# A hybrid diffusion trunk in one launch: the residual added by accumulating transfers, bare first sums, and the last stores and weight rows placed behind the operands

## The chip, the core and the metric

The kernel runs on one core of a Trainium2 chip. The metric is the device time of one execution in microseconds; times are given as the median of several runs with the lowest and the highest. A profile is one further execution, taken by the hardware profiler, with its own time.

The engines go by the names of the profile. PE is the matrix engine and PEld its weight load. DVE and ACT are the vector and the scalar engine. POOL and SP here only issue transfers. Each engine, and each queue of transfers, works through its own instructions in order.

## The reference, cut to what matters

One layer works on 640 tokens (512 latent, 128 context) of width 1024: a gated feed-forward half step, a token mixer, and a second half step.

```python
def swiglu(h, w1, w3, w2):
    return (jax.nn.silu(h @ w1) * (h @ w3)) @ w2
...
    x = x + 0.5 * m[2] * swiglu(hh, p['ffn1_w1'][l], p['ffn1_w3'][l], p['ffn1_w2'][l])
    hh = rmsnorm(x, g[1]) * (1 + m[4]) + m[3]
    y, ctx_out = token_mixer(hh, p, l, ctx)
    x = x + m[5] * y
    hh = rmsnorm(x, g[2]) * (1 + m[7]) + m[6]
    x = x + 0.5 * m[8] * swiglu(hh, p['ffn2_w1'][l], p['ffn2_w3'][l], p['ffn2_w2'][l])
```

The nine vectors `m` come from a conditioning vector times a 1024 by 9216 matrix. The inner width of the half steps is 2816. At its end the mixer adds two gated products, `sigmoid(gm) * (hm @ w_br_m) + sigmoid(gd) * (att @ w_br_d)`, and multiplies the sum by `w_out`.

## The kernel before, in words

Everything lies with features on the partitions, and the 640 tokens are two halves of 320 columns. Every product is done in three matmuls: weight and operand are split into a rounded high part and the remainder, and high by high, high by low and low by high are summed in PSUM (`mm3`, L159). ACT makes the high part (tile `ww`, `wB`, `wC` or `wH`), DVE the remainder.

**Half step.** The inner width is 11 blocks of 256. The two up products of a block are one weight granule each. From block 1 on each granule is done in seven products (Winograd's form of Strassen's algorithm, `products`, L375): the two halves of the tokens and of the inner dimension are added and subtracted beforehand, and so are the four quadrants of the weight. `parts` (L259) makes from the raw weight rows the tiles `wB` and `wC`, then the sums in place; `sums` (L277) makes `ww` of them. A product is 12 matmuls where a granule holds four row blocks. ACT copies running sums out of PSUM (`u`, `ps_f<-ps_f`) between the products, and the next product into that bank waits for the copy. The gated result of each block is stored to `g_dram` (`store_g`, L492).

**Down products.** The 11 blocks are summed in three groups, each for four output granules `j` of 256 features. In the first half step (`run_first`, L551) group 0 is blocks 0 to 3, done plainly (per `j` four units of 24 matmuls), group 1 is blocks 4 to 7 in seven products, group 2 the last three, plainly. In the second (`run`, L638) group 0 is blocks 0 to 2, plainly (units of 18 matmuls), and groups 1 and 2 are four blocks each in seven products. The operands of a group are fetched back from `g_dram` by `fetch` into tiles that the up products used (`S`, `hm`) or that lie free (`gA`, `SO`). An operand's fetch therefore waits until PE has used what lay there. Weight rows go to a ring of two `raw` buffers. Each unit's sum is scaled by the gate and added into the residual `x` by DVE (`add_residual`, L225). `x` had been read back to the core as four pairs of 640 KB (L1062 and L2305) while group 0 ran.

**Columns.** The conditioning matrix's columns are done on DVE, in 56 tiles (`Columns`, L730; `tile`, L747): each is a load of 512 KB on POOL's queue into `raw_a` or `ada` and two reductions, which DVE does wherever the program places the tile. At the mixer's end the tiles stand between the 16 units of `w_brd` (24 matmuls each) and the 16 of `w_brm`, with one buffer, so that a load can begin only when the tile before is done. `d_evac` (L2138) empties each `w_brd` unit's bank into `y`.

**What sets the order.** A planner with its own cost model lays down each engine's order; `issue_after` gives it an instruction to stay behind. On the chip each queue is in order and waits by semaphores. SP issues most transfers. POOL issues the column loads and some of the operand fetches, ACT one small load at the start.

## Time and profile before

| | us |
|---|---|
| median of 3 runs (lowest to highest) | 1839.37 (1837.65 to 1842.87) |
| the profiled execution | 1839.15 |
| its span, first to last instruction | 1837.4 |
| PE busy | 1800.9 (98%) |
| DVE busy | 1340.3 (73%) |
| ACT busy | 876.8 (48%) |
| POOL busy | 37.3 (2%) |
| bytes over the span | 166 GB/s, with HBM read 238.14 MB and written 67.56 MB |

A row of the waits says which engine waited for which, how long in total, how often, and the longest. A row of the timeline has the start, the length, engine, line, instruction and count; in brackets stands the idle time before it and what ended it. A row of stretches has its bounds, its length, then the busy time of PE, PEld, DVE, ACT and POOL with counts, the granted clock of PE (1.00 is full), the busy share of the transfer engines, and GB/s.

### The profile page before, as it was taken

To read this page: it belongs to the slowest core of one execution; us is meant where nothing else is said; L and a number is where in the kernel's file an instruction comes from. 1 tells how busy PE (TensorE), PEld (TensorE's weight loads), DVE (VectorE), ACT (ScalarE), POOL (GpSimd) and SP (SyncE) were. 2 spreads that over 40 slices of the span, in tenths; PEclk is the share of its full clock that TensorE was granted. 3 is DMA by queue.
4 is the path that set the end of the run, shared out by engine and by line. 5 is a ranking of instruction groups with operands and counts; after the bars stand their busy time and mean duration, and the time that the engine had idled before them with its cause. 6 is when DMAs were issued, how large, how long until landed. Compare 5 with 4: busy or idle time off the path is not lost. (4 is left out here: it accounts for less than half of the span.)

```text
span 1837.4 us, 30799 instructions
## 1 busy us (share of the span) xinstructions
PE 1800.9 (98%) x12622; PEld 1762.6 (96%) x12622; DVE 1340.3 (73%) x2188; ACT 876.8 (48%) x1510; POOL 37.3 (2%) x67
## 2 busy tenths in 40 slices
PE   8999999989999999999999999999899999999999
PEld 7999999989999999999999989999899999999999
DVE  6888996776986766475485558866767888896575
ACT  5655454123655454455555455672236545543232
POOL 0000000100000000000000000000000000000000
PEclk9999999989999999999999999999999999999999
DMA  8255567955234322112221155665552355658872
GB/s 332 100 197 190 182 218 275 358 212 198 82 137 140 122 67 86 62 62 94 73 91 68 42 165 179 238 213 191 201 173 79 132 173 191 204 187 297 312 292 81
DMA packets 130368, 307.71 MB, mean 167 GB/s; under 512 B 9841, under 2 KB 92017, under 8 KB 117297
## 3 DMA queue, kind: packets, MB, share of 16 engines
q1 hardware_dynamic: 119090, 259.06, 40.7%
q0 software_dynamic: 10992, 46.67, 6.8%
q8 instruction: 99, 1.62, 0.4%
q14 instruction: 43, 0.35, 0.1%
q10 hardware_dynamic: 144, 0.01, 0.0%
HBM read 238.14 MB, written 67.56 MB: 166 GB/s over the span
## 5 line engine op out<-in xcount | busy, mean ns | idle before, releaser
L75 PE MATMUL ps_f<-S,ww 128*128 128x320 f32 x2124 | 341.9, 310 | 2.5 <-DMA S<-g_dram 1.2
L75 PEld LDWEIGHTS ps_f<-S,ww 128*128 128x128 f32 x2124 | 319.1, 188 | 6.0 <-DVE ww L54 4.2
L75 PE MATMUL ps_p<-hH,wH 128*128 128x320 f32 x672 | 213.8, 318 | 6.8 <-DVE y L54 5.9
L75 PE MATMUL ps_f<-hm,ww 128*128 128x320 f32 x1272 | 203.5, 314 | 10.6 <-ACT u L51 6.4
L75 PE MATMUL ps_p<-hL,wH 128*128 128x320 f32 x672 | 208.8, 311 | 0.0
L75 PE MATMUL ps_p<-hH,wL 128*128 128x320 f32 x672 | 208.7, 311 | 0.0
L75 PEld LDWEIGHTS ps_f<-hm,ww 128*128 128x128 f32 x1272 | 193.8, 192 | 11.6 <-ACT u L51 6.6
L75 PE MATMUL ps_t<-wH,hH 128*128 128x256 f32 x640 | 185.2, 289 | 0.9 <-DVE x L57 0.9
L75 PE MATMUL ps_t<-wH,hL 128*128 128x256 f32 x640 | 181.0, 283 | 0.9 <-DVE hL L54 0.9
L75 PE MATMUL ps_t<-wL,hH 128*128 128x256 f32 x640 | 180.8, 283 | 0.0
L54 DVE TENSOR_TENSOR ww<-raw,ww 128x2048 fp32r<-128x2048 f32 (+1 forms) x67 | 150.2, 2241 | 32.9 <-ACT ww L51 32.7
L51 ACT ACTIVATE ww<-raw 128x2048 fp32r<-128x2048 f32 (+1 forms) x67 | 125.3, 1870 | 96.2 <-PE ps_f L75 57.2
L75 PE MATMUL ps_f<-hm,wB 128*128 128x320 f32 x960 | 153.8, 309 | 0.0
L54 DVE TENSOR_TENSOR raw<-raw 128x1024 f32<-128x1024 f32 x168 | 145.2, 864 | 1.8
L75 PEld LDWEIGHTS ps_f<-hm,wB 128*128 128x128 f32 x960 | 144.1, 188 | 0.0
L75 PEld LDWEIGHTS ps_p<-hH,wH 128*128 128x128 f32 x672 | 127.4, 190 | 7.8 <-DVE y L54 6.2
L75 PEld LDWEIGHTS ps_p<-hL,wH 128*128 128x128 f32 x672 | 127.3, 189 | 0.3
L51 ACT ACTIVATE u<-ps_f 128x320 f32<-128x320 f32 x117 | 50.7, 434 | 160.4 <-PE ps_f L75 160.2
L75 PEld LDWEIGHTS ps_p<-hH,wL 128*128 128x128 f32 x672 | 127.2, 189 | 0.0
L75 PEld LDWEIGHTS ps_t<-wH,hH 128*128 128x128 f32 x640 | 122.3, 191 | 1.5 <-ACT nsq L51 1.1
L75 PEld LDWEIGHTS ps_t<-wH,hL 128*128 128x128 f32 x640 | 122.3, 191 | 1.1 <-DVE hL L54 1.1
L75 PEld LDWEIGHTS ps_t<-wL,hH 128*128 128x128 f32 x640 | 122.5, 191 | 0.4
(306 smaller groups left out, 3445.8 us busy)
## 6 DMA issues: line engine op xcount, KB each, us to landing
g_dram<-g SPq DMA_DIRECT2D x44, 640.0 KB, 7.4
raw_a<-in_w_ada_c POOLq DMA_DIRECT2D x30, 512.0 KB, 4.3
g_dram<-g SPq DMA_DIRECT2D x24, 480.0 KB, 8.2
raw<-in_w1b SPq DMA_DIRECT2D x11, 1024.0 KB, 4.8
raw<-in_w3b SPq DMA_DIRECT2D x11, 1024.0 KB, 6.3
raw<-in_w1a SPq DMA_DIRECT2D x10, 1024.0 KB, 4.9
raw<-in_w3a SPq DMA_DIRECT2D x10, 1024.0 KB, 6.2
hm<-g_dram POOLq DMA_DIRECT2D x7, 1280.0 KB, 8.9
```

Source lines behind the costliest of these rows:

```text
L51: return placed(nc.scalar.activation(*args, **kw))
L54: return placed(eng.tensor_tensor(out=out, in0=in0, in1=in1, op=op))
L75: tc.keep_in_program_order(nc.tensor.matmul(*args, **kw))
```

## The change

Five things are altered.

1. `begin_sum` is new. In group 0 of both half steps ACT writes the scaled sum to `x` (a copy with the gate as scale), where DVE added it to a residual that had been read in. The four reads of `x` are gone. In group 1, POOL issues four accumulating transfers (`add_pair`), which add the residual's pairs 2, 3, 0 and 1 into `x`.
2. The stores of the last block, and the weight rows of the second output granule, are issued behind the fetches of group 0's operands. In the first half step these fetches go from POOL's queue to SP's and take another order of tiles.
3. In the first half step, group 1's operands A12 and S3 go from POOL's queue to SP's, A22 and S4 to ACT's queue, behind a copy of the first seven products. Group 2's get both `gA` and `SO`, from SP.
4. The columns are placed differently: 11 tiles in the first up products (10 before), then 9 during group 0 and 4 during group 2 (14 before, some of them during group 1). At the mixer's end 5 and 7 tiles take the place of 6 and 6, with two buffers each, every second unit, and each behind an emptied bank.
5. The weight parts of the next granules are kept behind the last `begin_sum`.

The diff, cut:

```diff
+    def begin_sum(x, ps, d, hf, gate):
+        c0 = hf * HALF
+        for s0, s1, j in SEGS[hf]:
+            ins = act(x[d][:, s0:s1], ps[:, s0 - c0 : s1 - c0], AF.Copy, scale=gate[:, d, j : j + 1])
+        return ins
...
+                    with ExitStack() as st:
+                        st.enter_context(tc.issue_after(gr.split_at))
+                        if i == 0 and self.begun is not None:
+                            st.enter_context(tc.issue_after(self.begun.ins))
                         work[i + 1][0].parts(self.fp)
...
-                    for i in range(2):
-                        nc.sync.dma_start(out=self.g_dram[c0:c1, :, i, b, :].rearrange("s p n -> p s n"), in_=g[:, i].bitcast(F32))
+                    def store(g=g, c0=c0, c1=c1):
+                        for i in range(2):
+                            nc.sync.dma_start(out=self.g_dram[c0:c1, :, i, b, :].rearrange("s p n -> p s n"), in_=g[:, i].bitcast(F32))
+
+                    if b == FB - 1:
+                        self.stores.append(store)
+                    else:
+                        store()
...
-                [up[i] for i in (S1, S2, A11, A12)],
-                [up[i] for i in (S3, S4, A22, S1, S2, A11, A12)],
-                [up[S3], None, up[S1], up[S2]],
+                [up[i] for i in (A11, S1, S2, A12)],
+                [up[i] for i in (S3, S4, A22, A11, S1, S2, A12)],
+                [up[S3], None, None, up[S1]],
...
+            second = down[0][1].load
+            down[0][1].load = lambda: None
+
+            def used_last(i):
+                if i in (A11, S1, S2, A12):
+                    ins = fetch(0, (A11, S1, S2, A12).index(i), nc.sync)
+                    if i == A12:
+                        with tc.issue_after(ins.ins):
+                            second()
+
+            work[-1][3] = used_last
...
+                if q == 0:
+                    self.begun = begin_sum(x, p, 2 * j + f, hf, gate)
+                else:
+                    self.at_vec = add_residual(x, p, 2 * j + f, hf, gate)
...
+                def used(i):
+                    if j == 3 and i in (A11, S3):
+                        fetch(2, {A11: 0, S3: 3}[i])
+                    elif (j, i) == (3, S2):
+                        freed()
...
-                loaded = self.loaded = (down[0][j + 2] if j < 2 else mid[j - 2][0]).load()
-                if 0 < j:
-                    with tc.issue_after(loaded):
-                        fetch(1, (A11, S1, S2)[j - 1], nc.sync)
+                loaded = (down[0][j + 2] if j < 2 else mid[j - 2]).load()
+                with tc.issue_after(loaded):
+                    if j == 0:
+                        for f in self.stores:
+                            f()
+                    for i in ((), (), (A11, S1), (S2,))[j]:
+                        fetch(1, i, nc.sync)
...
-                    mid[0][0].parts(self.fp)
-                    mid[0][0].sums()
+                    with tc.issue_after(self.begun.ins):
+                        mid[0].parts(self.fp)
+                        mid[0].sums()
...
                     if (j, hf) == (3, 0):
-                        fetch(1, A12)
-                        fetch(1, S3)
-            fetch(1, A22)
-            fetch(1, S4)
-
+                        fetch(1, A12, nc.sync)
+                        fetch(1, S3, nc.sync)
...
+                if (i, hf) == (0, 1):
+                    with tc.issue_after(self.copied.ins):
+                        fetch(1, A22, nc.scalar)
+                        fetch(1, S4, nc.scalar)
...
+                    for q, tag in ((1, "gA"), (2, "SO")):
+                        at[2][q] = self.fp.tile([128, 2, 3, HALF], F32R, tag=tag, name="op")
+                        with tc.issue_after(down[2][1].loaded):
+                            fetch(2, q, nc.sync)
...
-            work[-1][3] = lambda i: {A11: lambda: fetch(0, 0), S1: lambda: fetch(0, 1), S2: lambda: fetch(0, 2), A12: lambda: fetch(0, 3)}.get(i, nothing)()
+            second = down[1].load
+            down[1].load = lambda: None
+
+            def used_last(i):
+                if i in (A11, S1, S2, A12):
+                    ins = fetch(0, (A11, S1, S2, A12).index(i))
+                    if i == A12:
+                        with tc.issue_after(ins.ins):
+                            second()
...
-                    aside(len(work) + j, 0)
-                    for i in ((A11, S1), (S2, A12), (S3,), ())[j]:
+                    if j == 0:
+                        for f in self.stores:
+                            f()
+                        at[1] += [self.fp.tile([128, 2, 4, HALF], F32R, tag=tag, name="op") for tag in ("gA", "SO")] + [at[0][0], at[0][3]]
+                        at[2] = at[0][1:3] + at[1][:5]
+                    for i in ((), (A11, S1), (S2, A12), (S3,))[j]:
                         fetch(1, i)
...
-                        add_residual(x, p, 2 * j + f, hf, gate)
-                    if (j, hf) == (3, 0):
-                        for i in (A22, S4):
-                            fetch(1, i, nc.gpsimd)
+                        self.begun = begin_sum(x, p, 2 * j + f, hf, gate)
+                    if j == 3:
+                        fetch(1, (A22, S4)[hf], nc.gpsimd)
...
-            self.products(last, nothing, prepared=True)
+            def between_last(i, at):
+                if (i, at) in ((0, 1), (1, 0), (2, 0), (3, 0)):
+                    add_pair((2, 3, 0, 1)[i])
+
+            self.products(last, between_last, prepared=True)
...
-            columns.place(10, csil, load_columns)
+            columns.place(11, csil, load_columns)
...
-        def reload_x(g):
-            dma(box["x"][1][:, 2 * g : 2 * g + 2, :], a["x"][:, 2 * g : 2 * g + 2, :])
+        def add_pair(g):
+            ps = slice(2 * g, 2 * g + 2)
+            nc.gpsimd.dma_start(out=box["x"][1][:, ps, :], in_=a["x"][:, ps, :], accum_op=ALU.add)
+
+        def adds(i, at):
+            if (i, at) in ((24, 1), (25, 0), (26, 0), (27, 0)):
+                add_pair({24: 2, 25: 3, 26: 0, 27: 1}[i])
+
+        def freed():
+                t = hp.tile([128, 2, 2, 4, HALF], F32, tag="hL", name="ada").rearrange("p a b c n -> p (a b c n)")
+                raws[:] = [t[:, :D], t[:, D : 2 * D]]
+                junks[0] = t[:, 2 * D : 2 * D + D // 2].bitcast(BF16)
+                columns.place(4, places[0], load_columns_down)
 
...
-            if at == 0 and 20 <= i < 23:
-                with tc.issue_after(hs.loaded):
-                    reload_x(i - 19)
+            adds(i, at)
...
-                if at and i in (3, 4, 5, 7, 9, 11, 14, 15, 16, 17):
+                if at and i in (3, 4, 5, 6, 7, 9, 11, 14, 15, 16, 17):
...
-                    columns.place(14, places[0], load_columns, 4)
+                    junks[:] = [g[:, 2 * D :].bitcast(BF16)]
+                    columns.place(9, places[0], load_columns_down, 4)
...
-        TILES = {(20, 1): 1, (21, 0): 1, (21, 1): 2, (22, 0): 1, (22, 1): 2, (23, 0): 2, (23, 1): 1, (24, 1): 1, (25, 1): 1, (26, 1): 1, (28, 1): 1}
...
+        TILES = {(21, 0): 2, (21, 1): 2, (22, 0): 2, (22, 1): 1, (23, 0): 1, (23, 1): 1, (28, 0): 2, (28, 1): 1, (29, 0): 1}
...
-            tt(vec, y1[g][:, mt, half(hf)], p, t, ALU.mult)
+            ml_vec[0] = tt(vec, y1[g][:, mt, half(hf)], p, t, ALU.mult)
...
+    turn = ["ktok", "so"]
+
     def load_columns_so(src):
-        t = mp.tile([128, 2, T], F32, tag="so", name="raw_a").rearrange("p a t -> p (a t)")[:, :D]
+        turn.append(turn.pop(0))
+        t = mp.tile([128, 2, T], F32, tag=turn[0], name="raw_a", bufs=1 + (turn[0] == "ktok")).rearrange("p a t -> p (a t)")[:, :D]
         nc.gpsimd.dma_start(out=t, in_=src)
         return t, junk
...
-    columns.place(6, csil2, load_columns_so, 1)
-    while fill.q:
+    columns.place(5, csil2, load_columns_so, 2)
+    for k in range(11):
         fill.one()
-        if columns.n:
-            columns.tile()
+        if k % 2 == 0 and columns.n:
+            columns.tile(ml_vec[0])
...
-    columns.place(6, csil2, load_columns_pair, 1)
     with tc.tile_pool(name="gate", bufs=1, reuse_waits="tile") as gp:
+        junk = gp.tile([128, D], BF16, name="junk")
+        turn = [2, 3]
...
+            raw = pair("k", turn[0], "raw_a").rearrange("p a t -> p (a t)")[:, :D]
...
+        columns.place(7, csil2, load_columns_pair, 2)
...
+        fill.units(2)
         while fill.q:
             fill.units(2)
             if columns.n:
-                columns.tile()
+                columns.tile(ml_vec[0])
...
-    def reload_x2(g):
-        nc.sync.dma_start(out=x_pairs[g], in_=x2_dram[:, 2 * g : 2 * g + 2, :])
+    def add_pair(g):
+        nc.gpsimd.dma_start(out=x_pairs[g], in_=x2_dram[:, 2 * g : 2 * g + 2, :], accum_op=ALU.add)
...
-            reload_x2(0)
-        elif at == 0 and 20 <= i < 23:
-            reload_x2(i - 19)
```

Three places show how the engines' orders move. The first is ACT at the passage from group 0 to group 1 of the first half step. `ww`, `wB`, `wC` are parts of the next weights, `ps_f<-ps_f` and `u` the copies on which the seven products wait, `x<-ps_f,half_m` the new bare sums. Before:

```order
L51 ACTIVATE ww<-raw 128x2048
L51 ACTIVATE ps_f<-ps_f 128x320
L51 ACTIVATE ww<-raw 128x2048
L51 ACTIVATE u<-ps_f 128x320
L51 ACTIVATE wB<-raw 128x1024
L51 ACTIVATE wC<-raw 128x512
L51 ACTIVATE u<-ps_f 128x320
L51 ACTIVATE ps_f<-ps_f 128x320
```

And with the change:

```order
L51 ACTIVATE ww<-raw 128x2048
L51 ACTIVATE x<-ps_f,half_m 128x192
L51 ACTIVATE x<-ps_f,half_m 128x128
L51 ACTIVATE wB<-raw 128x1024
L51 ACTIVATE wC<-raw 128x512
L51 ACTIVATE ps_f<-ps_f 128x320
L51 ACTIVATE u<-ps_f 128x320
L580 DMA S<-g_dram_103 128x2x1280
L580 DMA hm<-g_dram_103 128x2x1280
L51 ACTIVATE ww<-raw 128x2048
L51 ACTIVATE u<-ps_f 128x320
L51 ACTIVATE wB<-raw 128x1024
```

The parts `wB` of the third weight granule stood ahead of the second copy `u` and now stand behind it; two operand fetches have come in ahead of `ww`.

The second is SP at the passage from the up products to group 0 of the second half step: `raw<-in_w2b` is half of a granule's weight rows, `g_dram<-g` a store, `hm` and `S` with 960 columns the four operands of group 0 (A11, S1, S2, A12 in this order). Before:

```order
L97 DMA raw<-in_w2b 128x3x256 x2
L505 DMA g_dram_14323<-g 128x4x320
L652 DMA S<-g_dram_14323 128x2x960
L505 DMA g_dram_14323<-g 128x3x320
L652 DMA S<-g_dram_14323 128x2x960
L97 DMA raw<-in_w2b 128x3x256 x2
L2306 DMA x<-x_dram 128x1280
L652 DMA hm<-g_dram_14323 128x2x960
L652 DMA S<-g_dram_14323 128x2x1280
```

And with the change:

```order
L695 DMA S<-g_dram_14326 128x2x960
L517 DMA g_dram_14326<-g 128x4x320
L517 DMA g_dram_14326<-g 128x3x320
L695 DMA S<-g_dram_14326 128x2x960
L695 DMA hm<-g_dram_14326 128x2x960
L97 DMA raw<-in_w2b 128x3x256 x4
L517 DMA g_dram_14326<-g 128x4x320
```

Two granules' rows and a read of `x` stood ahead of the fourth operand; the rows now stand behind it, and the read is gone.

The third is DVE at the end of the `w_brd` units: `y<-ps_p,sig` empties a unit's bank, `junk,mod<-raw_a,csil` is one of a column tile's two reductions. Before:

```order
L54 TENSOR_TENSOR y_13178<-ps_p,sig 128x320
L756 ISA junk,mod<-raw_a,csil 128x1024
L756 ISA mod 128x1
L756 ISA junk,mod<-raw_a,csil 128x1024
L756 ISA mod 128x1
L54 TENSOR_TENSOR y_13178<-ps_p,sig 128x320
L54 TENSOR_TENSOR wL<-raw,wH 128x2048
```

And with the change:

```order
L54 TENSOR_TENSOR y_13181<-ps_p,sig 128x320 x2
L813 ISA junk,mod<-raw_a,csil 128x1024
L813 ISA mod 128x1
L813 ISA junk,mod<-raw_a,csil 128x1024
L813 ISA mod 128x1
L54 TENSOR_TENSOR y_13181<-ps_p,sig 128x320 x2
L54 TENSOR_TENSOR wL<-raw,wH 128x2048
```

A whole tile stood ahead of the last bank's emptying; now one stands ahead of the last two, and its load has the second buffer.

## The prediction

> **What bounds the kernel now.** I read the page's busy shares first, then PE's waits, then the stretches around the longest of them.

> ```profile
> PE 1800.9 (98%) x12622; PEld 1762.6 (96%) x12622; DVE 1340.3 (73%) x2188; ACT 876.8 (48%) x1510; POOL 37.3 (2%) x67
> ```

> ```profile
> PE ps_f L75 <- ACT u L51: 6.4, 1, 6.4
> PE ps_p L75 <- DVE y L54: 5.9, 1, 5.9
> PE ps_f L75 <- DMA hm<-g_dram: 3.9, 1, 3.9
> ...
> PE ps_f L75 <- DMA S<-g_dram: 1.2, 1, 1.2
> ```

> PE is the bound, and no matmul is taken out. What can go is its idle time, 1837.4 - 1800.9 = 36.5 us, and what hangs on it. Three single waits make 16.2 us of that, a fourth 1.2; the change touches all four places. Each of the long ones costs more than its length:

> ```profile
> 382.50:388.80 6.30, 0.00 (x0) 0.00 (x0) 0.83 (x1) 1.92 (x4) 0.00 (x0) 0.65 0.95 338
> 388.80:395.10 6.30, 6.27 (x25) 6.27 (x26) 6.30 (x13) 0.31 (x1) 0.00 (x0) 0.53 0.02 6
> 1287.60:1293.50 5.90, 0.00 (x0) 0.00 (x0) 2.91 (x6) 0.00 (x0) 0.15 (x1) 0.91 0.40 164
> 1293.50:1299.50 6.00, 5.99 (x23) 5.99 (x24) 5.25 (x6) 0.00 (x0) 0.38 (x1) 0.52 0.64 212
> 1691.90:1695.90 4.00, 0.13 (x1) 0.00 (x0) 0.85 (x1) 0.00 (x0) 0.00 (x0) 0.91 1.03 416
> 1695.90:1701.90 6.00, 5.99 (x22) 5.99 (x23) 0.68 (x2) 0.00 (x0) 0.00 (x0) 0.50 1.02 401
> ```

> ```profile
> 327.75 7.20 PE L75 MATMUL ps_f<-S,ww 128*128 128x320 f32 x48
> 334.79 7.20 PE L75 MATMUL ps_f<-hm,ww 128*128 128x320 f32 x48
> ...
> 369.99 1.92 PE L75 MATMUL ps_f<-S,wB 128*128 128x320 f32 x12
> ...
> 388.83 6.42 PE L75 MATMUL ps_f<-hm,ww 128*128 128x320 f32 x24 [6.37 <-ACT u L51]
> ...
> 1293.51 0.64 PE L75 MATMUL ps_p<-hH,wH 128*128 128x320 f32 x1 [5.93 <-DVE y L54]
> ...
> 1695.91 2.77 PE L75 MATMUL ps_f<-hm,ww 128*128 128x320 f32 x9 [3.87 <-DMA hm<-g_dram]
> ```

> At full clock 48 matmuls take 334.79 - 327.75 = 7.04 us, 0.1467 each. In the stretch behind each wait the granted clock is 0.50 to 0.53, and 25, 23 and 22 matmuls take 6.30, 6.00 and 6.00 us where 3.67, 3.37 and 3.23 would do: 2.63, 2.63 and 2.77 us more. So the waits are worth 6.37 + 2.63 = 9.00, 5.93 + 2.63 = 8.56 and 3.87 + 2.77 = 6.64 us.

> [...]

> **First wait: weight rows in the first half step.** Group 1 begins at 369.99. I write t for that moment; a product of 12 matmuls takes 1.76 us.

> ```profile
> 386.88 1.06 ACT L51 ACTIVATE wB<-raw 128x1024 fp32r<-128x1024 f32 x1 [10.54 <-DMA raw<-in_w2a]
> ```

> ```profile
> 364.90 51.50 SPq L97 DMA_DIRECT2D raw<-in_w2a  x8
> ```

> ```profile
> q0 software_dynamic: 1808, 7.86, 70.5%
> q1 hardware_dynamic: 2105, 2.09, 20.5%
> ```

> ```profile
> DMA to landing us min/median/max: 15.0/18.2/21.5
> ```

> The rows ahead are the timeline of ACT and of SP's queue; the queues of transfers from 360 to 390, POOL's as q0 and SP's as q1, with packets, MB and share of the engines; and the landing times of the `raw` tiles issued in that stretch. The copy `u` for which PE waited stood behind `wB` in ACT's order, and `wB` waited 10.54 us for weight rows that SP had issued at 364.90 and that took up to 21.5 us. The two queue rows say why: POOL's queue moved 7.86 MB, four operand fetches and column loads, and SP's 2.09. With the change the third granule's rows stand on SP's queue behind A12 and S3 (1280 KB each) and on POOL's side no fetch is left. From PE's freeing of these places at t - 7, 2.6 MB and then 1 MB at the 400 GB/s of such stretches take 9.2 us, so the rows land by about t + 5. `u` is now ahead of `wB`; the next copy behind `wB` and `wC` is needed at t + 14.1 (eight products), so the rows may come as late as t + 12. I count the 9.00 us as gone.

> What comes instead: A22 and S4 are issued by ACT after the third product, at t + 5.7, and needed at t + 12.3 and t + 15.8. And ACT's issuing stands ahead of `ww`:

> ```profile
> 1686.02 0.56 SPq L652 DMA_DIRECT2D hm<-g_dram  x1
> ...
> 1689.71 6.76 SPq L97 DMA_DIRECT2D raw<-in_w2b  x2
> ```

> ```profile
> L54 DVE TENSOR_TENSOR ww<-raw,ww 128x2048 fp32r<-128x2048 f32 (+1 forms) x67 | 150.2, 2241 | 32.9 <-ACT ww L51 32.7
> L51 ACT ACTIVATE ww<-raw 128x2048 fp32r<-128x2048 f32 (+1 forms) x67 | 125.3, 1870 | 96.2 <-PE ps_f L75 57.2
> ```

> No row has such a fetch on ACT. SP's cost 0.56 us each where the engines are free and 6.76 for two where they are full. With the low price `ww` and its remainder are ready at t + 5.7 + 1.1 + 1.9 + 2.2 = t + 10.9, just when the seventh product needs them; with the high one 5.7 us later. I take the low one, since by then SP's queue is nearly empty, and 1.0 us in all for this passage with the first granule's `ww`, which is split late. The 1.2 us at the start of group 0 go: its first operand is now A11, freed first.

> **The bare sums and the adds.** In each half step 24 instructions leave DVE and come to ACT.

> ```profile
> L57 DVE SCALAR_TENSOR_TENSOR x<-ps_f,half_m,x 128x192 f32<-128x192 f32 (+2 forms) x108 | 44.0, 435 | 59.3 <-PE ps_f L75 59.1
> ```

> ```profile
> L51 ACT ACTIVATE u<-ps_f 128x320 f32<-128x320 f32 x117 | 50.7, 434 | 160.4 <-PE ps_f L75 160.2
> ```

> ```profile
> 360.00:390.00 30.00, 23.63 (x158) 23.37 (x157) 22.28 (x34) 4.89 (x7) 5.03 (x8) 0.91 0.91 333
> 390.00:402.00 12.00, 12.00 (x69) 12.00 (x69) 10.14 (x18) 3.73 (x5) 0.00 (x0) 0.80 0.01 2
> ```

> That is 24 x 0.435 = 10.4 us off DVE and as much on ACT, which is busy 4.89 of 30 us there; nothing of it is on PE's path unless ACT is held for longer than the eight banks last, six units of 3.5 us. The columns that leave group 1 take 2.4 us per tile (two reductions of 1.23 us, as under the second wait) off a DVE that is busy 10.14 of 12 us.

> An accumulating transfer has no row in this trace. Plain ones of its size and of half as much again (destination, source, queue, count, KB each, median us to landing; the first between 300 and 400, the second between 390 and 470):

> ```profile
> x<-in_x SPq DMA_DIRECT2D x3, 640.0 KB, 13.9
> ```

> ```profile
> S<-g_dram POOLq DMA_DIRECT2D x1, 960.0 KB, 5.5
> ```

> At best it takes less than the 5.5 us of a larger transfer, at worst twice 13.9, as it must read both sides: 27.8. The transfer engines are at 0.01 in the stretch 390 to 402, so I take some 8. Pairs 2 and 3 are not needed before t + 25, so they are hidden; on pairs 0 and 1 see the third rival.

> **Second wait: a column tile in the mixer.**

> ```profile
> 1290.55 1.23 DVE L756 CUSTOM_DVE_ANT_0 junk<-raw_a,csil 128x1024 bf16<-128x1024 f32 x1 [5.82 <-DMA raw_a<-in_w_ada_c]
> ...
> 1292.97 0.48 DVE L54 TENSOR_TENSOR y<-ps_p,sig 128x320 f32<-128x320 f32 x1
> ```

> DVE waited 5.82 us for a tile's load, spent 2.4 on it, and only then emptied the last bank, on which the next stage of PE waits. Now a load has a second buffer and two tiles' time, 14 us, to land. What stays is the emptying itself, 0.48, and its signals: 0.65. The gain is 7.9 us.

> **Third wait: A12 in the second half step.**

> ```profile
> 1672.23 1.53 SPq L97 DMA_DIRECT2D raw<-in_w2b  x2
> ...
> 1678.50 2.77 SPq L97 DMA_DIRECT2D raw<-in_w2b  x2
> 1681.32 1.58 SPq L2306 DMA_DIRECT2D x<-x_dram  x1
> 1683.00 1.53 SPq L652 DMA_DIRECT2D hm<-g_dram  x1
> ```

> ```profile
> 1683.00 12.86 DMA hm<-g_dram
> ```

> Two granules' rows (four times 384 KB) and a pair of `x` (640 KB), 2.23 MB, stood ahead of A12; at the 416 GB/s of the stretch above they are 5.4 us. Without them A12 lands at 1695.86 - 5.4 = 1690.5, ahead of the 1692.0 at which PE stopped. Next in line are the moved rows of granule 1: 768 KB, 1.9 us, to 1692.4, then 1.4 on ACT and 1.7 on DVE (by width, from the `ww` rows): 1695.5, and PE needs them at 1685.3 + 72 x 0.1467 = 1695.8. That is close; I take 0.3 us, at worst 2.

> **Sum.** 9.00 + 1.2 - 1.0 + 7.9 + 6.64 - 0.3 = 23.4 us. From the profiled execution's 1839.15, that is 1815.7; the median before is 0.2 us above that execution.

> **Rivals.** (1) ACT's queue holds the copies: at the high issuing price PE waits 5.7 us at t + 10.9 and the clock drops, 2.6: 1824. For it: the engines were full for 20 us before this point; against it: the adds and POOL's fetches have left.

> (2) The weight rows are late again. If they take 21.5 us from t - 5, they land at t + 16.4, 4.4 after the limit, with the clock 7.0: 1822.7. For it: ACT's fetches of 5 KB rows now share the engines with SP's rows of 1 KB. [...]

> (3) Slower: the adds hold POOL's queue. Pair 1's cannot start before granule 1's last sum, t + 29.9 (17 products); behind it on the same queue is group 2's first operand, needed at t + 49.3 and 5.5 us long. An add of over 13.9 us makes PE wait, in both half steps. At 27.8: 2 x (13.9 + 2.6) = 33 us, 1849. It outweighs the gain from 22.9 us on. Against it: the idle engines.

> (4) The change doesn't relieve the engines, as the adds read twice and the rest is the same bytes: waits one and three stay in other places, only the second and the 1.2 go: 1830.

> **Chances and range.** A measurement of this kernel tells about 0.3% from no change. Forecast 0.60, (1) 0.11, (2) 0.11, (4) 0.10, of which 0.04 end within 0.3%, (3) 0.06, and 0.02 for no change of another kind. So faster 0.88, same 0.06, slower 0.06. All rests at zero give 1813.7; to the other side I reach past (1) and (2): 1812 to 1828.

> **What would show it.** Right: no PE wait over 1 us on `u`, `y` or `hm`, a clock of 1.00 through all three places, DVE's wait for `raw_a` at the mixer's end under 1 us, x adds landing within 14 us. Wrong: a PE wait on `ps_f` with ACT or `S<-g_dram` behind it within 16 us of group 1's start, a wait on `ww` at the second granule of the last group 0, or an add of over 20 us.

## The result, and the profile after

The changed kernel takes 1822.02 us (median; 1819.74 to 1822.86) where the kernel before took 1839.93 in the same comparison (1837.65 to 1842.87): a ratio of 0.990 (95% interval 0.9883 to 0.9917), 17.9 us less. The prediction was 1815.7, 23.4 us less, with a range of 1812 to 1828. The profiled execution took 1821.74 us, with a span of 1820.0.

First the page's busy shares after, then PE's waits, longest first:

```profile
PE 1796.7 (99%) x12622; PEld 1757.6 (97%) x12622; DVE 1323.9 (73%) x2140; ACT 895.3 (49%) x1558; POOL 37.1 (2%) x65
```

```profile
PE ps_a L75 <- DMA raw_a<-in_w_ada_k: 3.6, 2, 1.8
PE ps_st L75 <- DVE P L54: 2.1, 1, 2.1
PE ps_f L75 <- ACT u L51: 1.6, 2, 1.2
...
PE ps_f L75 <- DMA S<-g_dram: 0.9, 1, 0.9
```

The waits of 6.4 on `u`, 5.9 on `y` and 3.9 on `hm` are gone. The longer of the two on `u` is new. It lies in the last weight granule of the second half step, and it looks like the old one: the copy `u` stands behind `wB` in ACT's order, and `wB` waits for weight rows (ACT, then PE; before, ACT waited 6.06 us in this place and PE not at all):

```profile
1777.08 1.06 ACT L51 ACTIVATE wB<-raw 128x1024 fp32r<-128x1024 f32 x1 [7.39 <-DMA raw<-in_w2b]
```

```profile
1779.03 2.02 PE L75 MATMUL ps_f<-op,ww 128*128 128x320 f32 x12 [1.16 <-ACT u L51]
```

PE's idle time fell from 36.5 to 1820.0 - 1796.7 = 23.3 us, and its busy time by 4.2 with the same 12622 matmuls, which is clock. The same passages in stretches, at the changed kernel's times:

```profile
382.50:388.80 6.30, 5.41 (x37) 5.10 (x36) 4.13 (x6) 1.90 (x3) 0.00 (x0) 1.00 1.03 394
388.80:395.10 6.30, 5.89 (x40) 5.63 (x39) 4.24 (x7) 4.14 (x5) 0.00 (x0) 1.00 0.20 63
1274.70:1280.60 5.90, 5.90 (x42) 5.90 (x41) 2.92 (x6) 0.00 (x0) 1.05 (x2) 1.00 0.82 252
1280.60:1286.60 6.00, 6.00 (x43) 6.00 (x42) 2.79 (x2) 1.91 (x1) 0.00 (x0) 1.00 1.01 379
1679.90:1683.90 4.00, 4.00 (x29) 4.00 (x29) 1.76 (x1) 2.05 (x3) 0.00 (x0) 1.00 1.07 388
```

PE is at full clock (1.00) in all three, and what it idles in the first is the 0.9 us on `S` and 0.4 on `u`. So the whole came out smaller for another reason. It shows when the start of the same matmul is read in the two timelines and the differences are taken from one to the next:

| start of | before | after | difference | step | forecast for the step |
|---|---|---|---|---|---|
| last product with the conditioning matrix, `ps_a` | 39.69 | 41.82 | +2.1 | +2.1 | 0 |
| group 1, first half step | 369.99 | 371.03 | +1.0 | -1.1 | |
| first matmul of the mixer, `ps_t` | 473.76 | 466.87 | -6.9 | -7.9 | -9.2, with the row above |
| first memory product, `ps_k` | 1069.59 | 1064.17 | -5.4 | +1.5 | 0 |
| last `ps_hT` | 1245.03 | 1241.78 | -3.3 | +2.2 | 0 |
| last sum of squares ahead of the second half step, `ps_ss` | 1408.72 | 1396.71 | -12.0 | -8.8 | -7.9 |
| last up product, second half step | 1683.51 | 1671.52 | -12.0 | 0 | 0 |
| end of the span | 1837.4 | 1820.0 | -17.4 | -5.4 | -6.3 |

Where the change works, the steps add up to -23.2, and the forecast for them was -23.4. The 5.8 us that are missing were lost in three passages that the change does not touch. The granted clock there (after; for each place the 3.41 us ahead and the stretch itself):

```profile
31.28:34.69 3.41, 1.62 (x15) 1.39 (x18) 3.17 (x7) 0.90 (x2) 0.00 (x0) 1.00 1.02 399
34.69:38.11 3.42, 3.42 (x19) 1.84 (x20) 1.46 (x3) 2.19 (x4) 0.00 (x0) 0.50 0.42 172
1000.66:1004.08 3.42, 2.45 (x20) 1.83 (x19) 3.42 (x7) 2.36 (x6) 0.00 (x0) 1.00 0.00 0
1004.08:1007.49 3.41, 3.41 (x13) 3.12 (x13) 2.76 (x7) 0.44 (x3) 0.00 (x0) 0.50 0.00 0
1065.52:1068.93 3.41, 1.35 (x12) 1.11 (x11) 1.63 (x4) 1.41 (x6) 0.00 (x0) 1.00 1.00 376
1068.93:1072.34 3.41, 3.41 (x14) 3.03 (x13) 1.14 (x3) 2.81 (x10) 0.00 (x0) 0.50 1.02 359
```

Each is one stretch of 3.41 us at half clock, at most 1.7 us lost, 5.1 in all. The second can be priced by itself: the passage from the mixer's first matmul to the first memory product is 1.5 us shorter in each of the five traces of this document that have no such stretch at this place (the two with one more unit placed there are left out), and the same to 0.04 us in the six others that have it. The trace of before has none there, though it has short waits in these places too (`P` 2.0 us against 2.1, `raw_a` 1.35 against 1.79). But for 2.3 us at its end, after PE's last product, it has all its half clock behind the three long waits:

```profile
384.44:394.68 10.24, 5.85 (x22) 5.85 (x23) 6.71 (x12) 2.23 (x4) 0.00 (x0) 0.50 0.40 138
...
1292.39:1299.21 6.82, 5.70 (x21) 5.70 (x22) 6.07 (x9) 0.00 (x0) 0.53 (x1) 0.50 0.54 177
...
1695.16:1701.99 6.83, 6.08 (x23) 6.08 (x24) 0.68 (x2) 0.00 (x0) 0.00 (x0) 0.50 1.02 403
```

10.24 is three times 3.41, the others twice. The starts lie whole steps apart in each execution: 1004.08 - 34.69 is 284.0 times 3.4133, 1068.93 - 1004.08 is 19.0 times, and before 1292.39 - 384.44 is 266.0 times. So in these two traces the granted clock changed only in steps of 3.41 us, and the steps lay elsewhere in each: 34.69 us is 10.2 steps from the span's start, 384.44 is 112.6. How the short waits lie in these steps went with whether half clock followed, as counted in the last section. The stretch ahead is not always one of idle time: 1000.66 to 1004.08 has PE busy for 2.45 us, with short matmuls that wait for operands from DVE and ACT.

### The profile page after: what moved, and what is told of

The parts are those of the page before. It is cut to its first block, busy times and chain, and to the rows that moved or that the text cites. A ratio compares the mean times of both kernels' runs of the same rounds, so it can differ in the third digit from the quotient of the medians.

```text
span 1820.0 us, 30810 instructions
## 1 busy us (share of the span) xinstructions
PE 1796.7 (99%) x12622; PEld 1757.6 (97%) x12622; DVE 1323.9 (73%) x2140; ACT 895.3 (49%) x1558; POOL 37.1 (2%) x65
## 2 busy tenths in 40 slices
DMA packets 130622, 307.69 MB, mean 169 GB/s; under 512 B 9841, under 2 KB 92017, under 8 KB 117553
## 3 DMA queue, kind: packets, MB, share of 16 engines
q10 hardware_dynamic: 688, 2.63, 0.4%
## 4 chain that ended last, share of the span: by engine, by line
PE 85%; DVE 7%; DMA 4%; ACT 3%; issue 1%; SPq 0%; DVEq 0%; ACTq 0%
PE ps_f L75 43%; PE ps_p L75 19%; PE ps_t L75 11%; PE sc L75 3%; PE ps_o L75 2%; PE ps_n L75 2%; DVE ww L54 2%; DMA raw<-in_w2b 2%; DMA raw_a<-in_w_ada_k 1%; PE ps_wT L78 1%; PE ps_u L75 1%; DVE junk L813 1%; PE ps_qkT L78 1%; DMA out_new_c<-Cn 1%; DMA S<-g_dram 0%
## 5 line engine op out<-in xcount | busy, mean ns | idle before, releaser
L75 PE MATMUL ps_f<-S,ww 128*128 128x320 f32 x2184 | 352.5, 310 | 2.8 <-DMA S<-g_dram 0.9
L75 PEld LDWEIGHTS ps_f<-S,ww 128*128 128x128 f32 x2184 | 327.5, 188 | 6.7 <-DVE ww L54 4.6
L75 PE MATMUL ps_p<-hH,wH 128*128 128x320 f32 x672 | 212.8, 317 | 1.4 <-DVE stage L61 0.7
L75 PE MATMUL ps_p<-hL,wH 128*128 128x320 f32 x672 | 208.0, 309 | 0.0
L75 PE MATMUL ps_p<-hH,wL 128*128 128x320 f32 x672 | 207.9, 309 | 0.0
L54 DVE TENSOR_TENSOR ww<-raw,ww 128x2048 fp32r<-128x2048 f32 (+1 forms) x67 | 150.2, 2242 | 63.6 <-ACT ww L51 63.5
L75 PE MATMUL ps_f<-hm,ww 128*128 128x320 f32 x1176 | 185.8, 309 | 0.4 <-DVE ww L54 0.3
L75 PE MATMUL ps_t<-wH,hH 128*128 128x256 f32 x640 | 185.2, 289 | 0.9 <-DVE x L57 0.9
L75 PE MATMUL ps_t<-wH,hL 128*128 128x256 f32 x640 | 181.0, 283 | 0.9 <-DVE hL L54 0.9
L75 PE MATMUL ps_t<-wL,hH 128*128 128x256 f32 x640 | 180.8, 283 | 0.0
L75 PEld LDWEIGHTS ps_f<-hm,ww 128*128 128x128 f32 x1176 | 175.7, 188 | 1.0 <-DVE ww L54 1.0
L75 PE MATMUL ps_f<-hm,wB 128*128 128x320 f32 x1008 | 161.5, 309 | 0.0
L51 ACT ACTIVATE ww<-raw 128x2048 fp32r<-128x2048 f32 (+1 forms) x67 | 125.4, 1871 | 57.8 <-DVE raw L54 33.4
L75 PEld LDWEIGHTS ps_f<-hm,wB 128*128 128x128 f32 x1008 | 151.3, 188 | 0.0
L54 DVE TENSOR_TENSOR raw<-raw 128x1024 f32<-128x1024 f32 x168 | 145.5, 866 | 1.9
L75 PEld LDWEIGHTS ps_p<-hH,wH 128*128 128x128 f32 x672 | 126.7, 189 | 2.2 <-ACT num L51 0.9
L75 PEld LDWEIGHTS ps_p<-hL,wH 128*128 128x128 f32 x672 | 126.6, 188 | 0.4
L75 PEld LDWEIGHTS ps_p<-hH,wL 128*128 128x128 f32 x672 | 126.4, 188 | 0.0
L51 ACT ACTIVATE u<-ps_f 128x320 f32<-128x320 f32 x117 | 50.6, 433 | 153.7 <-PE ps_f L75 153.6
L75 PEld LDWEIGHTS ps_t<-wH,hH 128*128 128x128 f32 x640 | 122.3, 191 | 1.5 <-ACT nsq L51 1.1
L75 PEld LDWEIGHTS ps_t<-wH,hL 128*128 128x128 f32 x640 | 122.3, 191 | 1.1 <-DVE hL L54 1.1
L75 PEld LDWEIGHTS ps_t<-wL,hH 128*128 128x128 f32 x640 | 122.5, 191 | 0.4
```

What stands on the lines that cost most here:

```text
L51: return placed(nc.scalar.activation(*args, **kw))
L54: return placed(eng.tensor_tensor(out=out, in0=in0, in1=in1, op=op))
L75: tc.keep_in_program_order(nc.tensor.matmul(*args, **kw))
```

## The experiments

Times are medians beside runs of the kernel before on the same chip, whose medians were 1840.0 to 1840.4 (1839.93 beside the changed kernel).

**The mixer's end alone.** The kernel before with `load_columns_so` in turns of two buffers, every second unit, 5 and 7 tiles (the edit, cut):

```diff
-    columns.place(6, csil2, load_columns_so, 1)
-    while fill.q:
+    columns.place(5, csil2, load_columns_so, 2)
+    for k in range(11):
         fill.one()
-        if columns.n:
-            columns.tile()
+        if k % 2 == 0 and columns.n:
+            columns.tile(ml_vec[0])
```

> The kernel before with the change's placing of the column tiles at the mixer's end alone (5 and 7 tiles with two buffers, every second unit). The prediction's second term, read again with the changed kernel's trace, where the passage became 8.8 us shorter: PE's 5.9 us wait on y goes, the stretch at half clock behind it too, and the time falls from 1839.9 by about 8 to 9 us, to 1831. The waits on u (6.4) and on hm (3.9) stay. Rival: the tiles wait for their loads in another place, and only 3 to 4 us come out. Beside it: the changed kernel's trace has half clock in three stretches of 3.41 us that the trace of before does not have (from 34.7, 1004.1 and 1068.9 us), in code that the change doesn't touch. If they are a matter of chance they turn up or not in this kernel too; if the change made them by its other parts, none does.

1833.12 against 1840.33, a ratio of 0.9962 (0.9950 to 0.9974): 7.2 us less, 4.8 to 9.2 by the interval. PE's longest waits there:

```profile
PE ps_f L75 <- ACT u L51: 5.6, 1, 5.6
PE ps_f L75 <- DMA hm<-g_dram: 3.7, 1, 3.7
```

The wait on `y` is gone and the other two stand. The second term holds by itself. The two that stand were followed by two and one half-clock stretches, where the profile of before has three and two. None of the three half-clock stretches of the changed kernel is in this trace, but there is one from 11.56 us, in the opening, which neither kernel had.

**Part 1 undone, and then by pieces.** In the changed kernel (the edit, cut; the reads are issued where they stood before):

```diff
-                    self.begun = begin_sum(x, p, 2 * j + f, hf, gate)
+                    self.begun = add_residual(x, p, 2 * j + f, hf, gate)
...
-            nc.gpsimd.dma_start(out=box["x"][1][:, ps, :], in_=a["x"][:, ps, :], accum_op=ALU.add)
+            dma(box["x"][1][:, ps, :], a["x"][:, ps, :])
```

> The changed kernel with its first part undone: the residual is read back by four plain reads on SP's queue as before, DVE adds every sum of group 0 to it, and no adding transfer is issued. Everything else as in the changed kernel. My theory, that the order of the transfers cured the first and the third wait, expects at most the reads' own price, 1.6 us for each 640 KB that stands ahead of weight rows or an operand at 410 GB/s: 1822 to 1826. The rival, that taking the reads and the sums off SP and DVE is what cured them, expects the first wait (9.0 with its clock) and the third (6.6) back in some form: 1830 to 1838.

1833.57: 11.5 us of the gain go, and the rival was right. PE waited 3.8 and 1.7 us for `ww` at the passage to group 1, and 5.6 in the second half step. (The profiled execution is the longest of the eight, 1840.03; 4.7 us of what it has above the changed kernel lie in the mixer, which the edit does not touch.) Which piece of part 1 is it? First DVE's work:

```diff
-            ins = act(x[d][:, s0:s1], ps[:, s0 - c0 : s1 - c0], AF.Copy, scale=gate[:, d, j : j + 1])
+            ins = placed(vec.tensor_scalar(out=x[d][:, s0:s1], in0=ps[:, s0 - c0 : s1 - c0], scalar1=gate[:, d, j : j + 1], scalar2=None, op0=ALU.mult))
```

> The changed kernel, but the 24 bare sums of each group 0 are written by DVE (a product with the gate) and not by ACT. No read of the residual comes back, the adding transfers stay. It tells apart what made the kernel without part 1 11.5 us slower than the changed one (1833.6 against 1822.0). If it was DVE's work, which lies behind the column tiles and ahead of the weights' sums, this one is as slow: 1831 to 1835, with PE waiting for ww at the passage to group 1 in both half steps. If it was the four reads of the residual on SP's queue, this one is as fast as the changed kernel: 1822 to 1823.

1822.33: whether ACT or DVE writes the sums makes no difference in the time that shows. In the trace PE did wait 0.79 and 1.77 us for `ww` at the passage to group 1, and the clock fell for one stretch. Then the reads, issued as in the run without part 1, with sums and adds as changed (`reload_x` at its old places again):

> The changed kernel with the four reads of the residual kept on SP's queue in both half steps, in the order of the run without part 1, but their values are not used: the bare sums still overwrite them and the adding transfers stay. The sums by DVE cost nothing by themselves (1822.3), the run without part 1 cost 11.5 us. If the reads do it (their bytes and their places on SP's queue), this one is slow too: 1830 to 1834. If it was DVE, whose additions then stood between the column tiles and waited for the reads, so that ten tile reductions were left behind 355 us (five in the changed kernel), this one pays at most the bytes, 1.6 us for each of two reads near a tight place: 1822 to 1825.

1838.64, 16.6 us more than the changed kernel and the same as before (ratio 0.9993, 0.9981 to 1.0006). So it is the reads. Against the changed kernel's profile, 3.5 us of the loss come between the conditioning products and the mixer, and 13.5 of the 15.7 in all come after the last up product of the second half step. PE there (timeline of this run):

```profile
1727.75 2.46 PE L75 MATMUL ps_f<-op,ww 128*128 128x320 f32 x12 [2.83 <-DMA op<-g_dram]
...
1750.38 0.90 PE L75 MATMUL ps_f<-hm,ww 128*128 128x320 f32 x2 [3.23 <-ACT ww L51]
```

With 1.52 and 1.43 more for `ww` that is 9.0 us of waiting, and three stretches of half clock. No column tile is left on DVE by then (the last ends at 1650.9). What has come is on SP's queue: the last read alone kept SP for 6.05 us at 1691.99, and the operands `op`, whose issuing took SP from 1693.85 to 1703.86 in the changed kernel, were issued from 1699.01 to 1709.56. DVE in the first half step:

```profile
356.71 1.23 DVE L54 TENSOR_TENSOR wB<-raw,wB 128x1024 fp32r<-128x1024 f32 x1 [6.70 <-ACT wB L51]
...
373.22 1.22 DVE L814 CUSTOM_DVE_ANT_0 ada<-ada,csil 128x1024 bf16<-128x1024 f32 x1
...
375.50 1.22 DVE L814 CUSTOM_DVE_ANT_0 ada<-ada,csil 128x1024 bf16<-128x1024 f32 x1
...
381.51 2.29 DVE L54 TENSOR_TENSOR ww<-raw,ww 128x2048 fp32r<-128x2048 f32 x1 [0.86 <-ACT ww L51]
```

With the reads the planner lays nine tile reductions behind `wB` (at 356.7), four of them behind 370 us, among the parts of which the next `ww` is made (two are shown). DVE sat idle for 6.70 us ahead of `wB` and then had them in the way; PE waited 1.88 and 1.77 us for `ww`, and the clock fell. That is little more than in the run before (0.79 and 1.77), which has no reads, so this half step is not where the reads cost most. How much of the rest is the reads' bytes and how much the order of what stands behind them could not be told apart: both come with the reads.

The other way round, part 1 alone on the kernel before:

> The kernel before with part 1 of the change alone: bare sums by ACT, no reads of the residual, four adding transfers on POOL's queue in each group 1; the order of the other transfers and the column tiles as before. The prediction's steps give it only what the missing 640 KB ahead of A12 are worth, 1.6 us of the third wait and at most as much again of its clock: 1837 to 1838.7. The rival reading of the run without part 1, that taking the sums off DVE is worth 11 us by itself, expects 1829. Against the adds: if they hold up POOL's queue, it is slower than before, over 1841.

1837.69, a ratio of 0.9990 (0.9980 to 1.0000), 2.3 us less, just within the noise, and within what the prediction's steps give; the wait on `hm` was 2.3 instead of 3.9. So the parts are worth little apart: the adds 2.3 us, all else without them 6.8 (the mixer's end alone makes 7.2), together 17.9.

**The first wait: who moves the operands.** The changed kernel with `fetch(1, A12)`, `fetch(1, S3)`, `fetch(1, A22)`, `fetch(1, S4)` on POOL's queue again:

> The changed kernel with group 1's four operand fetches of the first half step (A12, S3, A22, S4) back on POOL's queue, at the places in the program where they stood before; nothing is issued by ACT. My theory of the first wait: POOL's queue takes the larger share of the transfer engines, so the third granule's weight rows, which landed 12.5 us behind group 1's start in the changed kernel, land about 16 us behind it as before; ACT's wB waits and PE idles 3 to 5 us there, with the clock 6 to 8: 1828 to 1830. The rival: what cured the wait is that the copy u now stands ahead of wB in ACT's order, and the rows would have been early enough in any case: 1822, no PE wait over 1.5 us there.

1826.10, 4.1 more. Queues from 360 to 390 in this run, and the rows' landing:

```profile
q0 software_dynamic: 1334, 6.34, 67.0%
q1 hardware_dynamic: 2112, 2.10, 21.4%
```

```profile
DMA to landing us min/median/max: 12.9/13.5/14.0
```

The third granule's two transfers of rows, issued at 371.1 and 371.5, landed up to 385.5, which is 15.9 us behind this run's group 1 (369.58); with the change, 12.5. PE idled 3.23 + 1.77 = 5.0 us for `ww`. Landing and wait are as the theory had them (16 us, 3 to 5 us), and so is the passage: it was 6.6 us longer than in the changed kernel's profile. The whole came to less, since the opening was 2.1 us shorter there; the clock held in it. The five times (1823.0 to 1828.0) all lie above the changed kernel's four, though the two intervals overlap a little. The rival's forecast, no wait over 1.5 us, failed. But that the late rows made PE wait is not shown, for with the edit the planner also laid `wB` behind two more copies (ACT):

```profile
380.40 0.42 ACT L51 ACTIVATE ps_f<-ps_f 128x320 f32<-128x320 f32 x1 [1.38 <-PE ps_f L75]
385.62 0.44 ACT L51 ACTIVATE u<-ps_f 128x320 f32<-128x320 f32 x1 [4.80 <-PE ps_f L75]
385.95 1.05 ACT L51 ACTIVATE wB<-raw 128x1024 fp32r<-128x1024 f32 x1
```

Even with early rows `wB` would have begun at 385.95. The rows landed 15.9 us behind group 1's start with the fetches on POOL's queue and 12.5 us behind it without; whether the rows or ACT's order cost the 5.0 us stays open. A later variant has the same wait: with the kernel of one more unit (below) and ACT's two fetches 5 us earlier,

> The kernel with one more unit ahead of the memory heads (1819.6) in which ACT issues the fetches of A22 and S4 in the first half step at the start of group 1, behind the last bare sum, and not behind the copy u of the third product. They go 5 us earlier, so the wait for S (0.9 to 1.2 us) goes; in exchange they share the engines with the third granule's weight rows, and wB has moved behind two more copies in ACT's order. If the operands were the tight ones, 1818.3 to 1819; if the rows are, PE waits for ww at the third granule and 1821 or more.

it took 1823.28, 3.7 more than without, and PE waited 3.2 and 1.4 us for `ww`, while the wait on `S` went. So A22 and S4 were not what held this passage. Here too the rows came late (up to 385.6) and `wB` stood behind the same two copies, until 386.07.

**The third wait: what stands ahead of A12.**

```diff
             def used_last(i):
+                if i == A12:
+                    second()
                 if i in (A11, S1, S2, A12):
-                    ins = fetch(0, (A11, S1, S2, A12).index(i))
-                    if i == A12:
-                        with tc.issue_after(ins.ins):
-                            second()
+                    fetch(0, (A11, S1, S2, A12).index(i))
```

> The changed kernel with the second granule's weight rows in the second half step issued ahead of the operand A12, as before the change (768 KB of rows of the next two granules come ahead of it twice); the residual's read stays out. In the changed kernel A12 was issued at 1667.75, landed 10.2 us later, at 1677.95, and PE wants it 6.8 us behind the start of group 0 at 1673.3, at 1680.1: a margin of 2.1 us. At 416 GB/s 1.54 MB take 3.7 us, so PE waits 1.6 us for A12, with up to 1.7 for the clock: 1823.6 to 1825.5, and a wait of PE on hm with a transfer behind it. The rival, that the read of the residual alone made A12 late before, expects no such wait and 1822.

1825.58, 3.6 more; the two intervals overlap (0.9900 to 0.9932, and 0.9883 to 0.9917), so the time alone does not show it. The chain of this run from 1670 to 1700, and PE's wait:

```profile
1668.88 12.54 DMA hm<-g_dram
```

```profile
PE ps_f L75 <- DMA hm<-g_dram: 2.1, 1, 2.1
```

A12 landed at 1681.42, 3.5 us later than in the changed kernel. The forecast from the bytes was 3.7, so the rows' place is worth what their bytes say in landing. PE's wait came out at 2.1 for 1.6, with the clock full. The rest of the 4.1 us that this profile lost after the last up product lies in the last granule: the wait on `u` was 2.0 us there and not 1.2, and one stretch of half clock followed it.

**The adds.** Price and limit. First with `accum_op=ALU.add` left out:

> The changed kernel with the eight adding transfers made plain: same places, sizes and queue, but the residual overwrites the sums of group 0, so these sums are left out of the result. It prices the adding. In the changed kernel the eight landed 5.8 to 11.2 us after their issue, median 7.3 in the first half step and 8.9 in the second. If adding costs (it must read both sides), the plain ones land in half to two thirds of that, 4 to 5 us; if the way through the queue is what takes the time, in the same 6 to 9 us. The whole time stays at 1822 either way, as nothing waits for them.

Issue to landing of the four in each half step, in this run:

```profile
x<-in_x POOLq DMA_DIRECT2D x4, 640.0 KB, 5.0
...
x<-x_dram POOLq DMA_DIRECT2D x4, 640.0 KB, 7.0
```

and in the changed kernel:

```profile
x<-in_x POOLq DMA_DIRECT2D x4, 640.0 KB, 7.3
...
x<-x_dram POOLq DMA_DIRECT2D x4, 640.0 KB, 8.9
```

Adding cost some 2 us on 640 KB (1.5 to 2.9, pair by pair). The one execution took 1816.59, 3.1 us under the changed kernel's lowest, where no difference had been expected; 2.1 us of it are the opening, in which the clock held. One execution is too little to call the rest the adds' price. But one wait tells more: the 1.16 us on `u` in the last granule of the second half step. All ten profiles of kernels with adding transfers have it, at 1.0 to 2.0 us; with plain transfers it is 0.17, and the three without transfers into `x` in group 1 (the kernel before, the mixer's end alone, part 1 undone) do not have it. So the adds do reach PE there. By which way they make the weight rows late was not followed.

Then the limit, with pair 1's add of the first half step issued three times:

> The changed kernel with the fourth adding transfer of the first half step (pair 1) issued three times, and group 2's two operands on POOL's queue kept behind them; the residual's pair 1 is counted three times in the result. The third rival, made to happen: the add was issued at 406.8 and takes 7 to 11 us, each next one waits for the one before, so group 2's first operand is issued at some 422 to 426 and not at 408.5, lands 9 us later, and PE, which wants it at 422.5, idles 8 to 12 us, with 2 to 3.4 for the clock: 1832 to 1837. If adds don't hold the queue: 1822.

1838.98 (the profiled one 1833.7), a little above what was expected. POOL's queue and PE in this run:

```profile
416.29 0.89 POOL L1122 DMA_DIRECT2D x<-in_x  x1 [3.11 <-DMA x<-in_x]
424.82 0.87 POOL L1122 DMA_DIRECT2D x<-in_x  x1 [7.64 <-DMA x<-in_x]
425.37 1.54 POOL L580 DMA_DIRECT2D S<-g_dram  x2
```

```profile
434.37 2.74 PE L75 MATMUL ps_f<-S,ww 128*128 128x320 f32 x9 [13.79 <-DMA S<-g_dram]
```

The third rival exists: POOL stood 3.11 and 7.64 us until an add had landed where the next one wants the same tile, the operand behind them was issued at 425.37, and PE waited 13.79 us for it. In the changed kernel no add is followed by one to the same tile, and the queue went on before the add had landed (POOL, after):

```profile
406.79 0.86 POOL L1121 DMA_DIRECT2D x<-in_x  x1 [8.12 <-DVE x L57]
408.48 0.74 POOL L580 DMA_DIRECT2D S<-g_dram  x1 [0.83 <-PE ps_f L75]
```

The add took 11.2 us to land, but the operand was issued 1.7 us behind it, when PE had freed its place. It landed at 421.9, and PE wanted it at 422.5.

**The clock.** Twelve idle matmuls, ones times ones into an unused part of the bank, where PE waits 1.8 us for a load at 33 us and the granted clock was 0.50 from 34.69 to 38.11:

```diff
                 ps = psum.tile([128, 512], F32, tag="mm", name="ps_a")
+                if k == 6:
+                    for _ in range(12):
+                        mm(ps[:, 256:384], ones, ones, start=True, stop=True)
```

> [...] The theory that the clock is set for 3.41 us at a time by how much PE did in the 3.41 us before expects 1.00 throughout 30 to 45 us and the time 1.7 us lower in executions that had the drop: 1820.3 to 1822. The rival, that the clock there has another cause, expects 0.5 again at 34 to 38 us and 1822 to 1823.6, as the idle matmuls end later than the load when that comes early.

1822.16, no difference. The clock held at 33 us and the mean granted clock of its four executions was 0.9993, against 0.9978 for the changed kernel, but the last `ps_a` came at 40.7, against 39.7 to 40.5 in traces without the drop and 41.8 to 42.0 with it. The twelve stand in the trace as 24 matmuls that end at 35.2, 2.8 us for a wait of 1.8. So that `ps_a` was 1.1 to 1.3 us earlier than where the clock dropped, and 0.2 to 1.0 later than where it held. Real work is better filling: one more unit of the gate products ahead of the memory heads,

```diff
     with written():
-        fill.units(2)
+        fill.units(3)
```

> The changed kernel with one more unit of 24 matmuls of the gate products (3.5 us of work that otherwise comes later) ahead of the first head's memory products in the mixer, where PE waits 1.7 to 2.3 us for P in every profile so far and the granted clock was then 0.5 for 3.41 us in two of six. If PE's idle time there is what costs, the wait and the drop go: 1818.5 to 1820.3. The rival, that the chain of DVE and ACT through the memory heads sets this passage, expects the time back as waits on num at the end of it: 1822 or more.

took 1819.59 (1818.58 to 1822.87), with no half-clock stretch in its trace:

```profile
1060.00:1080.00 20.00, 18.38 (x112) 16.62 (x111) 10.28 (x30) 13.09 (x38) 0.00 (x0) 1.00 0.78 267
```

Its ratio to before is 0.9895 (0.9878 to 0.9912). By the medians it is 2.4 us faster than the changed kernel, but the two intervals overlap, so this is likely and not shown.

## Why the prediction came out as it did

**The three waits.** Place and price were right, and so was the cause of the second and the third. The second (-8.8 against -7.9) and the third (-5.4 against -6.3) are each within 1 us, and each came back, or went, in a run of its own. What the third step lacks is about the new wait on `u` of 1.16 us, which lies in the same row of the table.

**The first wait.** -9.0 against -9.2 for the passage, but not as the prediction had it. It let the weight rows land at t + 5; they landed at t + 12.5. They were issued at t + 1.5, because SP waited there 7.8 us for DVE to be done with the buffer, and the step counted only the operands ahead of them. That is half a microsecond behind the limit of t + 12 that the same part worked out, so that the step held by luck more than by its sum. PE lost nothing to it that shows: ACT had done the rows' `wB` and the copy behind it by 385.45 and then idled 4.77 us for PE, and the 0.41 us on `u` came only at 392.51. ACT's issuing, which had no row, cost 0.60 and 0.64 us (timeline after):

```profile
376.51 0.60 ACTq L580 DMA_DIRECT2D S<-g_dram  x1
377.14 0.64 ACTq L580 DMA_DIRECT2D hm<-g_dram  x1
...
383.54 1.06 ACT L51 ACTIVATE wB<-raw 128x1024 fp32r<-128x1024 f32 x1 [3.08 <-DMA raw<-in_w2a]
```

That is the price that the prediction took. But it is not the price of free transfer engines, as the prediction had read it: their share was 1.03 from 375 to 378 us, and it had been 1.04 from 1684 to 1688 in the kernel before, where SP's 0.56 was read. The first rival is out; the second, late rows, came within a microsecond of being true.

**Bare sums and adds.** "Nothing of it is on PE's path" was right for the 24 instructions, but the adds put 1.0 to 2.0 us on it in the last granule, and the sentence left out the reads. Their bytes were counted in the third wait alone, at 1.6 us; that fits the old order (2.3 us measured), but in the new one their absence carries 11.5 to 16.6 us. The fourth rival, that the change relieves nothing because the bytes stay the same, is out. That an add reads both sides was an assumption of the prediction, and the bytes do not show it: the transfers of a whole execution come to 307.69 MB with adding and with plain ones. The adds were taken at 8 us; they landed in 6.1 to 11.2. The third rival's limit of 13.9 us was too high: it took 5.5 us for group 2's first operand, which needed 13.4, and let pair 1's add start at t + 29.9, where it started at t + 35.8. That operand had 0.6 us to spare, so a queue held until the add's landing at 418.0 would have cost PE some 9 us by that landing time (an estimate). It did not happen because the queue went on 1.7 us behind the add's issue, and not because the adds were short.

**The signs.** The waits on `y` and `hm`, the clock in the three places and the adds' landing came as stated. Three signs did not: the wait on `u` of 1.16 us is over 1; DVE waited 2.44 and 1.87 us for `raw_a` at the mixer's end, where under 1 had been named (PE did not wait for it); and the 0.90 us on `S`, within 16 us of group 1's start, is one of the signs named for being wrong. None is large.

**The sum.** The term that was mis-sized is the clock, 2.63 + 2.63 + 2.77 = 8.0 us. The forecast took it all out, as if the clock would be full everywhere afterwards. Net it gave 4.2: PE's busy time fell by that much. By the mean granted clock of the executions, which is known for the unprofiled ones too, before has 0.9937 (53 executions), 2 x 0.0063 x 1838 = 23 us at half clock, 6.8 stretches; the changed kernel 0.9978 (4), 8 us, 2.4 stretches (estimates, with 0.50 as the only clock below 1.00, as in both traces). (This mean takes in the span's end too, where PE has no work left: 2.3 us of half clock in the profiled execution before, 0.1 after.) In the profiled execution before, seven stretches lay behind the three waits and none elsewhere. In the ten experiments with the mixer's early part unchanged, the passages that no edit touches had 1, 3, 1, 1, 2, 1, 3, 2, 2 and 0 stretches. So one execution's account of the clock was read as the kernel's: it put three, two and two stretches behind the waits and none anywhere else.

Of the idle time, 13.2 us went where 15.4 were forecast: a load in the opening came 0.4 us later, and the waits on `S`, `u` and `num` are 3.2 us together, where 1.95 had been allowed for.

## What to carry to other kernels

Here a wait's price was its idle time and a number of half-clock stretches that was not the same in two traces (three and two behind the wait on `u`, two and one behind that on `hm`); read the first from one profile, the second from the mean clock of many, and expect some of it to come back elsewhere (of 8.0 us behind the three waits 4.2 stayed away). Parts that reorder queues and parts that remove transfers should be judged together: here neither half gave much without the other. Before a transfer is counted as early, look for the buffer it fills, not only for what stands ahead of it on its queue.

## What was not expected of the hardware

An adding transfer of 640 KB took some 2 us more than a plain one (median 7.3 against 5.0 us in the first half step, 8.9 against 7.0 in the second). Issuing a fetch from ACT cost it 0.60 to 0.64 us with the transfer engines full (a share of 1.03 from 375 to 378 us).
